# Low part of one weight tile in four made by ScalarE's negated high part and an accumulating DMA, not by VectorE

## The chip, the cores and the metric

The kernel runs on one core of a Trainium2 chip. The core has a matrix engine (TensorE, PE in the profile; its weight loads are PEld), VectorE (DVE), ScalarE (ACT), GpSimd (POOL) and SyncE (SP), which here only issues transfers, and sixteen DMA engines that move data between HBM and SBUF, the on-chip memory. Matrix products land in PSUM. Each engine works through its own queue in order and waits at an instruction until the semaphores named there have come. The metric is the device time of one execution in microseconds (us).

## What is computed

A decoder trunk for 256 tokens of width 2048: one layer of gated linear attention (GLA), one layer of stick-breaking attention, each followed by a SwiGLU block of inner width 5632, and a final norm. Nearly all of the work is in products of the activations with large weight matrices in float32:

```python
a = rmsnorm(h, attn_norm_w[layer])
h = h + gla_mixer(a, gla_w_in, ...)              # layer 0: 2048 x 6160 in, 2048 x 2048 out
# layer 1: a @ sb_w_q, kv @ sb_w_kv, stick-breaking attention, o @ sb_w_out
h = h + swiglu(rmsnorm(h, ffn_norm_w[layer]), ffn_w_gate_up[layer], ffn_w_down[layer])

def swiglu(h, w_gate_up, w_down):
    gate, up = jnp.split(h @ w_gate_up, 2, axis=-1)
    return (jax.nn.silu(gate) * up) @ w_down
```

## The kernel before

The product in float32 is made of three products in the faster format float32r. Each operand is split into a high part, which is the value rounded to 12 bits, and a low part, which is the value minus the high part; hi x hi, hi x lo and lo x hi are summed in PSUM.

All weights come through `load_w` in tiles of 128 x 1024 (512 KB). SP issues the load into a buffer `raw` (line 115), ACT makes `hi` by a rounding copy (line 119), and DVE makes `lo` as raw minus hi (line 120). There are four raw buffers (pool `wraw`) and three each of hi and lo (pool `wsp`). The next load into a raw buffer must wait until it was read for the last time; the next hi and lo must wait until PE has read the old ones. 787 tiles are loaded in all; four of them, in `gemm_tok_in_turn`, have hi and lo in a larger buffer that is handed in as `dst`.

`gemm_tok` uses a tile as the moving operand: two rows of blocks (j), two token tiles (t), three products, so twelve matmuls of 512 columns per tile (line 137). It serves the GLA gate and values, all of the SwiGLU products, the attention values and the output projections. `gemm_col` uses a tile as the stationary operand (lines 169, 170 and 172): sixteen matmuls per tile. It serves q, k and the decay of the GLA layer, and k and q of the attention layer. `inv_rms` makes a small power on POOL (line 211), and `gemm_col` ends with a scaling on POOL (line 176).

The order of the instructions on each engine, and which buffer a tile gets, is laid down by a scheduler when the program is built; it moves matmuls a little against the order of the source.

Of the kernel before, what the change touches and what calls it, by code (L numbers as in the profile page):

```python
# [1 line left out]

# [6 lines left out]
F32 = mybir.dt.float32  # L9
# [4 lines left out]
ALU = mybir.AluOpType  # L14
PSUM = bass.MemoryType.PSUM

P = 128
D = 2048
S = 256
NT = S // P  # L20
# [22 lines left out]
def trunk_kernel(  # L43
# [20 lines left out]
    v, a, pe, g = nc.vector, nc.scalar, nc.tensor, nc.gpsimd  # L64
# [7 lines left out]
    ps_tr = ctx.enter_context(tc.tile_pool(name="ps_tr", bufs=2, space=PSUM))  # L72
    ps_x = ctx.enter_context(tc.tile_pool(name="ps_x", bufs=2, space=PSUM))

    # residual stream, token on the partition
    h = const.tile([P, NT, D], F32, name="h")

    def load_x(nb):
        for t in range(NT):
            nc.sync.dma_start(h[:, t, nb * NB : (nb + 1) * NB], x[t * P : (t + 1) * P, nb * NB : (nb + 1) * NB])  # L80

# [1 line left out]
    ident = const.tile([P, P], F32, name="ident")  # L83
    make_identity(nc, ident)
    ones = const.tile([P, P], F32, name="ones")
# [21 lines left out]
    def gain(key, k):  # L107
        return gains[:, col[key] + k : col[key] + k + 1]

# [1 line left out]
    def load_w(ap, k0, nk, c0, ncol, dst=None):  # L111
        raw = wraw.tile([P, 1024], F32, name="raw")
        hi, lo = dst or (wsp.tile([P, 1024], F32R, name="hi"), wsp.tile([P, 1024], F32R, name="lo"))
        n = nk * ncol
        nc.sync.dma_start(
            raw[:, :n].rearrange("p (k c) -> p k c", k=nk),
            ap[k0 * P : (k0 + nk) * P, c0 : c0 + ncol].rearrange("(k p) c -> p k c", p=P),
        )
        a.copy(hi[:, :n], raw[:, :n])  # L119
        v.tensor_tensor(lo[:, :n], raw[:, :n], hi.bitcast(F32)[:, :n], ALU.subtract)  # L120
        return (hi[:, :n].rearrange("p (k c) -> p k c", k=nk), lo[:, :n].rearrange("p (k c) -> p k c", k=nk))

    def gemm_tok(w_ap, kt, lhs, c0, evac, k_row0=0, before=None):
        """out[token, 512 columns from c0]: activations stationary, weights moving."""
        acc = [ps_acc.tile([P, NB], F32, name="acc") for _ in range(NT)]
        k0 = 0
        while k0 < kt:
            nk = 1 if before is not None and k0 < 2 else 2
            hi, lo = load_w(w_ap, k_row0 + k0, nk, c0, NB)
            if before is not None:  # L130
                before(k0)
            for j in range(nk):
                k = k0 + j
                for t in range(NT):
                    xh, xl = lhs(k, t)
                    for n, (l, r) in enumerate(((xh, hi), (xh, lo), (xl, hi))):
                        pe.matmul(acc[t], l, r[:, j, :], start=(k == 0 and n == 0), stop=(k == kt - 1 and n == 2))  # L137
            k0 += nk
        for t in range(NT):
            evac(t, acc[t])  # L140

    def gemm_tok_in_turn(w_ap, kt, lhs, c0, evac, k_row0):
        """gemm_tok with the block of weights held, so that the first token tile is done before the second."""
        wh, wl = (w.rearrange("p (n a) s c -> p n (a s c)", n=8)[:, i : i + 4] for w in xt_pair()[2:] for i in (0, 4))
        parts = []
        for i, k0 in enumerate(range(0, kt, 2)):
            parts.append(load_w(w_ap, k_row0 + k0, 2, c0, NB, (wh[:, i, :], wl[:, i, :]) if i < 4 else None))
        for t in range(NT):
            acc = ps_acc.tile([P, NB], F32, name="acc")
            for k in range(kt):  # L150
                xh, xl = lhs(k, t)
                hi, lo = (w[:, k % 2, :] for w in parts[k // 2])
                for n, (l, r) in enumerate(((xh, hi), (xh, lo), (xl, hi))):
                    pe.matmul(acc, l, r, start=(k == 0 and n == 0), stop=(k == kt - 1 and n == 2))  # L154
            evac(t, acc)

    def gemm_col(w_ap, c0, nct, xhl, dst, scale):
        """dst[column, 256 tokens] for nct column tiles from c0, times scale: weights stationary, activations moving."""
        nk = 1024 // (nct * P)
        acc = [ps_acc.tile([P, NB], F32, name="acc") for _ in range(nct)]  # L160
        for k0 in range(0, KD, nk):
            hi, lo = load_w(w_ap, k0, nk, c0, nct * P)
            for j in range(nk):
                both = xhl[:, k0 + j].rearrange("p s c -> p (s c)")
                first, last = k0 + j == 0, k0 + j == KD - 1
                for c in range(nct):
                    cs = slice(c * P, (c + 1) * P)
                    if not last:
                        pe.matmul(acc[c], hi[:, j, cs], both, start=first, stop=False)  # L169
                    pe.matmul(acc[c][:, :S], lo[:, j, cs], xhl[:, k0 + j, 0, :], start=False, stop=False)  # L170
                    if last:
                        pe.matmul(acc[c], hi[:, j, cs], both, start=False, stop=True)  # L172
        for c in range(nct):
            a.copy(dst[:, c, :], acc[c][:, S:])
            v.tensor_tensor(dst[:, c, :], acc[c][:, :S], dst[:, c, :], ALU.add)
        g.tensor_tensor(dst, dst, scale.rearrange("p (n c) -> p n c", n=1).broadcast_to([P, nct, S]), ALU.mult)
# [3 lines left out]
        return t[:, :, 0, :], t[:, :, 1, :], t  # L180

    def split_scaled(dst_h, dst_l, src, scale):
        """dst_h + dst_l = src * scale, with scale per partition."""
        a.mul(dst_h, src, scale)  # L184
        v.scalar_tensor_tensor(dst_l, src, scale, dst_h.bitcast(F32), ALU.mult, ALU.subtract)  # L185

    def make_xt(src, nb, dsts):
        """Transposes 512 columns of both token tiles, and splits them times each gain."""
        for j0 in (0, 2):
            tp = ps_tr.tile([P, 512], F32, name="tr")  # L190
            for j in (j0, j0 + 1):
                for t in range(NT):
                    o = (j - j0) * S + t * P
                    pe.transpose(tp[:, o : o + P], src(t)[:, j * P : (j + 1) * P], ident)  # L194
            for j in (j0, j0 + 1):
                k = nb * 4 + j
                for key, kk, xh, xl in dsts:
                    split_scaled(xh[:, k, :], xl[:, k, :], tp[:, (j - j0) * S : (j - j0 + 1) * S], gain(key, kk + (j if key == "gnorm" else k)))
# [3 lines left out]
        a.activation(junk, src, AF.Square, accum_out=ss)  # L202

    def inv_rms(ss, n, name):
        """ss [P, NT, parts] -> (sum / n + eps) ** -0.5, [P, NT]"""
        nt = ss.shape[1]
        s = stat.tile([P, nt], F32, name=f"{name}_s")
        v.tensor_reduce(s, ss, axis=mybir.AxisListType.X, op=ALU.add)
        v.tensor_scalar(s, s, 1.0 / n, EPS, ALU.mult, ALU.add)
        r = stat.tile([P, nt], F32, name=f"{name}_r")  # L210
# [1 line left out]
        return r  # L212

    def along_tokens(r, name):
        """r [token, NT] -> [P, 256], the same row on every partition."""
        dg = stat.tile([P, NT, P], F32, name="diag", bufs=1)
        bp = ps_tr.tile([P, 512], F32, name="tr")
        for t in range(NT):
# [9 lines left out]
        make_xt(lambda t: h[:, t, nb * NB : (nb + 1) * NB], nb, dsts)  # L228

    def residual_gemm(w_ap, kt, lhs, k_row0, after=None, after_tile=None):  # L230
        """h += lhs @ w, 512 columns at a time."""
        for nb in range(NCB):
            def evac(t, acc, nb=nb):
                hs = h[:, t, nb * NB : (nb + 1) * NB]
# [42 lines left out]

                residual_gemm(w_dn, 4 * len(blocks), hid_lhs, blocks[0] * 4, **(after if blocks is PASSES[-1] else {}))

    # ================= layer 0: gated linear attention =================  # L280
    w_in = gla_w_in[0]
    ah, al, ahl = xt_pair()
    a_lhs = lambda k, t: (ah[:, k, t * P : (t + 1) * P], al[:, k, t * P : (t + 1) * P])
# [2 lines left out]
    load_x(0)  # L286

    with tc.tile_pool(name="gla", bufs=1) as gp:
        # output gate input, first block: the input arrives, is summed and transposed alongside
        rg = gp.tile([P, NT, VW], F32, name="rg")  # L290
        ss = stat.tile([P, NT, NCB], F32, name="ss")
        r0 = None
# [24 lines left out]
        rq_bc = stat.tile([P, S], F32, name="rq_bc", bufs=1)  # L317
        v.tensor_scalar(rq_bc, r0_bc, GDK**-0.5, None, ALU.mult)

        # masks within one tile of 128: earlier token by the later halves of a level's blocks, and the diagonal  # L320
        HP = P // 2
        mk = gp.tile([P, len(LEVELS) - 1, HP], U8, name="mk")
        mf = gp.tile([P, HP], F32, name="mf")
# [7 lines left out]
        v.tensor_copy(mk_d, ident)  # L331

        tc.keep_in_program_order(a.preload_act_table_set("natural_log_exp_and_others"))
        # log decay, [key dim, token]
        gl = gp.tile([P, 1, S], F32, name="gl")
        gemm_col(w_in, GIN - P, 1, ahl, gl, r0_bc)
        wgu = gp.tile([P, QKW], F32, name="wgu", tag="vt", bufs=2)
# [17 lines left out]
        for k in range(GKT):  # L355
            v.tensor_tensor_scan(B[:, k, :], B[:, k, :], ab[:, k, :], 0.0, ALU.add, ALU.subtract)  # L356

        # q and k, [key dim, token]
        qt = gp.tile([P, GKT, S], F32, name="qt")
        kt = gp.tile([P, GKT, S], F32, name="kt")  # L360
        for dst, c0, sc in ((qt, 0, rq_bc), (kt, QKW, r0_bc)):
            for pr in range(GKT // 2):
                gemm_col(w_in, c0 + pr * 2 * P, 2, ahl, dst[:, 2 * pr : 2 * pr + 2, :], sc)

        # scores, [earlier token, later token]: pairs split by the smallest aligned block that holds both
        sc_in = gp.tile([P, GH, NT, P], F32, name="sc_in")
        sc_x = gp.tile([P, GH, P], F32, name="sc_x")
        v.memset(sc_in, 0.0)
# [86 lines left out]
    ss = stat.tile([P, NT, NCB], F32, name="ss")  # L455
    ffn(0, fh, fl, r1, after=lambda nb, ss=ss: norm_block(ss, nb, [("kv", 0, kh, kl), ("attn1", 0, qh, ql)]))

    # ================= layer 1: stick-breaking attention =================
    r2 = inv_rms(ss, D, "n")
    r2_bc = along_tokens(r2, "r_bc")  # L460
    rq_bc = stat.tile([P, S], F32, name="rq_bc", bufs=1)
# [3 lines left out]
    with tc.tile_pool(name="sb", bufs=1) as sp_:  # L465
# [5 lines left out]
        v.tensor_copy(tri_r, upto)  # L471
        ones_r = sp_.tile([P, P], F32R, name="ones_r")
        v.tensor_copy(ones_r, ones)
        # two heads side by side: earlier tile 0 with all later tokens, then earlier tile 1 with later tile 1
        ZA, ZW = 2 * S, 3 * S
        pen = sp_.tile([P, ZW], F32, name="pen")
        g.memset(pen, 0.0)
# [12 lines left out]
        def attend(pr, qp):  # L490
# [5 lines left out]
            z = sp_.tile([P, ZW], F32, name="z", bufs=2)  # L496
            v.tensor_tensor(z[:, :ZA], za, pen[:, :ZA], ALU.add)
            v.tensor_tensor(z[:, ZA:], zb[:, :S], pen[:, ZA:], ALU.add)
            # -log_sigmoid(-z) = max(z, 0) + log(1 + exp(-|z|))
            e = sp_.tile([P, ZW], F32, name="e", bufs=2)  # L500
            a.activation(e, z, AF.Abs)
            a.activation(e, e, AF.Exp, scale=-1.0)
# [3 lines left out]
            fl_ = sp_.tile([P, ZW], F32R, name="fl", bufs=2)  # L506
            a.copy(fh_, e)
            v.tensor_tensor(fl_, e, fh_.bitcast(F32), ALU.subtract)
            # sums over the later keys and the key itself
            ca = ps_tr.tile([P, 512], F32, name="tr")  # L510
            cb = ps_tr.tile([P, 512], F32, name="tr")
            pe.matmul(ca, tri_r, fh_[:, :ZA], start=True, stop=False)
# [84 lines left out]
```

## Time and profile before

| | |
|---|---|
| median of 2 runs | 2282.19 us (2281.15 to 2283.24) |
| the profiled execution, first to last instruction | 2279.7 us |
| PE busy | 2263.7 us, 99% |
| PEld busy | 1891.0 us, 83% |
| DVE busy | 1238.5 us, 54% |
| ACT busy | 1046.4 us, 46% |
| POOL busy | 60.4 us, 3% |
| moved by the DMA engines | 419.23 MB, mean 184 GB/s |

The profile is that of one execution. "L120" is line 120 of the kernel. A row of the timeline has its start, its duration, the engine, the line, the operation, what it writes and reads, and in brackets how long the engine was idle before and what ended that. The end of a matmul is modelled: the next one starts before it ends. The granted clock of TensorE stands as a share of full speed.

### The profile page before, as it was taken

To read this page: it belongs to the slowest core of one execution; us is meant where nothing else is said; L and a number is where in the kernel's file an instruction comes from. 1 tells how busy PE (TensorE), PEld (TensorE's weight loads), DVE (VectorE), ACT (ScalarE), POOL (GpSimd) and SP (SyncE) were. 2 spreads that over 40 slices of the span, in tenths; PEclk is the share of its full clock that TensorE was granted. 3 is DMA by queue.
4 is the path that set the end of the run, shared out by engine and by line. 5 is a ranking of instruction groups with operands and counts; after the bars stand their busy time and mean duration, and the time that the engine had idled before them with its cause. 6 is when DMAs were issued, how large, how long until landed. Compare 5 with 4: busy or idle time off the path is not lost.

```text
span 2279.7 us, 27154 instructions
## 1 busy us (share of the span) xinstructions
PE 2263.7 (99%) x10658; PEld 1891.0 (83%) x10658; DVE 1238.5 (54%) x1251; ACT 1046.4 (46%) x1222; POOL 60.4 (3%) x72
## 2 busy tenths in 40 slices
PE   9999999999999999999999999999999999999998
PEld 7888878888888888888888888888888888888887
DVE  6766455545545545544664567655445444554555
ACT  6544444444434443344554446554444344434444
POOL 2100000000000000000000111000000000000000
PEclk9999999999999999999999999999999999999999
DMA  7554555666666666666566654556666666666664
GB/s 224 169 164 143 153 166 181 188 188 190 188 193 193 189 189 193 194 186 193 185 186 194 186 185 141 167 184 191 186 192 190 193 190 192 186 194 193 191 188 157
DMA packets 242712, 419.23 MB, mean 184 GB/s; under 512 B 12972, under 2 KB 64264, under 8 KB 242456
## 3 DMA queue, kind: packets, MB, share of 16 engines
q1 hardware_dynamic: 242408, 416.44, 60.5%
q8 instruction: 83, 1.36, 0.2%
q10 hardware_dynamic: 176, 1.06, 0.1%
q14 instruction: 45, 0.37, 0.0%
HBM read 415.35 MB, written 2.10 MB: 183 GB/s over the span
## 4 chain that ended last, share of the span: by engine, by line
PE 99%; DVE 0%; issue 0%; DMA 0%; ACT 0%; SPq 0%; POOLq 0%; POOL 0%; DVEq 0%; ACTq 0%
PE acc L137 82%; PE acc L169 7%; PE acc L170 4%; PE px L397 1%; PE tr L264 1%; PE tr L194 1%; PE acc L172 0%; PE acc L154 0%; PE px L494 0%; PE tr L525 0%; PE px L439 0%; DMA raw<-in_gla_w_in_dram 0%; DVE B L356 0%; PE px L409 0%; PE tr L526 0%
## 5 line engine op out<-in xcount | busy, mean ns | idle before, releaser
L120 DVE TENSOR_TENSOR lo<-raw,hi 128x1024 fp32r<-128x1024 f32 (+1 forms) x783 | 972.1, 1243 | 938.4 <-ACT hi L119 937.9
L119 ACT CAST hi<-raw 128x1024 fp32r<-128x1024 f32 (+1 forms) x783 | 823.7, 1052 | 1043.1 <-PE acc L137 904.3
L137 PE MATMUL acc<-hi,xhl 128*128 128x512 f32 x4096 | 1274.7, 391 | 0.8 <-ACT xhl L184 0.8
L137 PEld LDWEIGHTS acc<-hi,xhl 128*128 128x128 f32 x4096 | 769.4, 188 | 161.1 <-issue 1.9
L137 PE MATMUL acc<-lo,xhl 128*128 128x512 f32 x2048 | 799.9, 391 | 0.0
L137 PEld LDWEIGHTS acc<-lo,xhl 128*128 128x128 f32 x2048 | 385.1, 188 | 78.7
L137 PE MATMUL acc<-lo,hid_h 128*128 128x512 f32 x680 | 264.9, 390 | 0.0
L137 PE MATMUL acc<-hi,hid_l 128*128 128x512 f32 x680 | 264.6, 389 | 0.0
L169 PE MATMUL acc<-xhl,hi 128*128 128x512 f32 x735 | 256.1, 396 | 0.6 <-ACT hi L119 0.6
L137 PE MATMUL acc<-hi,hid_h 128*128 128x512 f32 x680 | 240.7, 390 | 0.0
L170 PE MATMUL acc<-xhl,lo 128*128 128x256 f32 x784 | 209.6, 281 | 2.1 <-DVE lo L120 2.0
L169 PEld LDWEIGHTS acc<-xhl,hi 128*128 128x128 f32 x735 | 134.8, 188 | 27.7 <-ACT hi L119 1.0
L170 PEld LDWEIGHTS acc<-xhl,lo 128*128 128x128 f32 x784 | 147.7, 189 | 8.8 <-DVE lo L120 3.0
L137 PEld LDWEIGHTS acc<-hi,hid_l 128*128 128x128 f32 x680 | 127.7, 188 | 26.5
L137 PEld LDWEIGHTS acc<-hi,hid_h 128*128 128x128 f32 x680 | 127.6, 188 | 26.3
L137 PEld LDWEIGHTS acc<-lo,hid_h 128*128 128x128 f32 x680 | 127.6, 188 | 26.1
L184 ACT ACTIVATE xhl<-tr,gains 128x256 fp32r<-128x256 f32 x96 | 40.9, 470 | 28.2 <-PE tr L194 20.9
L185 DVE SCALAR_TENSOR_TENSOR xhl<-tr,gains,xhl 128x256 fp32r<-128x256 f32 x96 | 42.4, 478 | 13.0 <-ACT xhl L184 13.0
L235 DVE TENSOR_TENSOR h<-acc,h 128x512 f32<-128x512 f32 x64 | 41.2, 682 | 7.6 <-PE acc L154 5.2
L258 ACT ACTIVATE sg<-acc,n_r 128x512 f32<-128x512 f32 x44 | 30.0, 690 | 20.8 <-PE acc L137 20.8
L267 ACT CAST hid_h<-tr 128x512 fp32r<-128x512 f32 x44 | 23.6, 589 | 31.4 <-PE tr L264 31.4
L268 DVE TENSOR_TENSOR hid_l<-tr,hid_h 128x512 fp32r<-128x512 f32 x44 | 28.3, 686 | 17.3 <-ACT hid_h L267 17.3
(153 smaller groups left out, 709.1 us busy)
## 6 DMA issues: line engine op xcount, KB each, us to landing
raw<-in_ffn_w_gate_up_dram SPq DMA_DIRECT2D x352, 512.0 KB, 3.9
raw<-in_ffn_w_down_dram SPq DMA_DIRECT2D x176, 512.0 KB, 3.7
raw<-in_gla_w_in_dram SPq DMA_DIRECT2D x97, 512.0 KB, 3.9
raw<-in_sb_w_kv_dram SPq DMA_DIRECT2D x64, 512.0 KB, 3.9
raw<-in_gla_w_out_dram SPq DMA_DIRECT2D x32, 512.0 KB, 3.7
raw<-in_sb_w_q_dram SPq DMA_DIRECT2D x32, 512.0 KB, 3.6
raw<-in_sb_w_out_dram SPq DMA_DIRECT2D x32, 512.0 KB, 3.7
h<-in_x_dram SPq DMA_DIRECT2D x8, 256.0 KB, 5.7
```

What stands on the lines that cost most here:

```text
L119: a.copy(hi[:, :n], raw[:, :n])
L120: v.tensor_tensor(lo[:, :n], raw[:, :n], hi.bitcast(F32)[:, :n], ALU.subtract)
L137: pe.matmul(acc[t], l, r[:, j, :], start=(k == 0 and n == 0), stop=(k == kt - 1 and n == 2))
L169: pe.matmul(acc[c], hi[:, j, cs], both, start=first, stop=False)
L170: pe.matmul(acc[c][:, :S], lo[:, j, cs], xhl[:, k0 + j, 0, :], start=False, stop=False)
L184: a.mul(dst_h, src, scale)
L185: v.scalar_tensor_tensor(dst_l, src, scale, dst_h.bitcast(F32), ALU.mult, ALU.subtract)
L194: pe.transpose(tp[:, o : o + P], src(t)[:, j * P : (j + 1) * P], ident)
L235: v.tensor_tensor(hs, acc, hs, ALU.add)
L258: a.activation(sg[t], acc, AF.Silu, scale=r[:, t : t + 1])
L267: a.copy(hh[:, :, ts], tv)
L268: v.tensor_tensor(hl[:, :, ts], tv, hh.bitcast(F32)[:, :, ts], ALU.subtract)
```

## The change

In every fourth tile of those without `dst` (195 of 783), `lo` is no longer made by DVE. ACT writes minus `hi` into `lo`, and POOL then issues a DMA that reads `raw` and adds it to what stands in `lo`. The other tiles are as before. The rest of the diff takes out comments, so that line numbers move by up to seven.

```diff
+from itertools import count
...
+    tiles = count()
+
     def load_w(ap, k0, nk, c0, ncol, dst=None):
         raw = wraw.tile([P, 1024], F32, name="raw")
         hi, lo = dst or (wsp.tile([P, 1024], F32R, name="hi"), wsp.tile([P, 1024], F32R, name="lo"))
...
         a.copy(hi[:, :n], raw[:, :n])
-        v.tensor_tensor(lo[:, :n], raw[:, :n], hi.bitcast(F32)[:, :n], ALU.subtract)
+        if dst is None and next(tiles) % 4 == 3:
+            a.mul(lo[:, :n], hi.bitcast(F32)[:, :n], -1.0)
+            g.dma_start(lo[:, :n], raw[:, :n], accum_op=ALU.add)
+        else:
+            v.tensor_tensor(lo[:, :n], raw[:, :n], hi.bitcast(F32)[:, :n], ALU.subtract)
```

On ACT, at the start of the first product with `ffn_w_down` in layer 0, the casts followed each other before (the numbers tell the tiles apart; hi, lo and raw of one tile have numbers that follow each other):

```order
L119 CAST hi_4685<-raw_4684 128x1024
L119 CAST hi_4703<-raw_4702 128x1024
L119 CAST hi_4721<-raw_4720 128x1024
L119 CAST hi_4739<-raw_4738 128x1024
L119 CAST hi_4761<-raw_4760 128x1024
```

In the changed program the same place on ACT reads:

```order
L122 CAST hi_4734<-raw_4733 128x1024
L124 ACTIVATE lo_4735<-hi_4734 128x1024
L122 CAST hi_4753<-raw_4752 128x1024
L122 CAST hi_4771<-raw_4770 128x1024
L122 CAST hi_4789<-raw_4788 128x1024
L122 CAST hi_4811<-raw_4810 128x1024
L124 ACTIVATE lo_4812<-hi_4811 128x1024
```

Behind every fourth cast now stands the multiplication that writes minus hi into lo, ahead of the next tile's cast.

On PE, the matmuls of that same changed tile (hi_4734, lo_4735) in the changed program, behind the last one of the tile before it (hi_4716):

```order
L144 MATMUL acc_4659<-hi_4716,hid_l_3705 128x512
L144 MATMUL acc_4658<-hi_4734,hid_h_4022 128x512
L144 MATMUL acc_4659<-hi_4734,hid_h_4022 128x512
L144 MATMUL acc_4658<-lo_4735,hid_h_4022 128x512
L144 MATMUL acc_4658<-hi_4734,hid_l_4023 128x512
L144 MATMUL acc_4659<-lo_4735,hid_h_4022 128x512
```

The order is that of the program before at this place (hi, hi, lo, hi, lo); in 166 changed tiles of this form, and in 23 of the form of `gemm_col`, two matmuls with hi stand ahead of the first with lo, in the other six one, and no matmul of a later tile is put between them.

On SP, the loads at the same place before, with the semaphores each waits for (DMAHW is an earlier transfer that SP issued, DVE the last reader of the raw buffer):

```order
L115 DMA raw<-in_ffn_w_down_dram 128x2x512 [waits DMAHW7_49,DVE_49]
L115 DMA raw<-in_ffn_w_down_dram 128x2x512 [waits DMAHW0_49,DVE_49]
L115 DMA raw<-in_ffn_w_down_dram 128x2x512 [waits DMAHW1_49,DVE_49]
L115 DMA raw<-in_ffn_w_down_dram 128x2x512 [waits DMAHW2_49,DVE_49]
L115 DMA raw<-in_ffn_w_down_dram 128x2x512 [waits DMAHW3_49,DVE_49]
```

And now (DMASW is a transfer that POOL issued):

```order
L118 DMA raw<-in_ffn_w_down_dram 128x2x512 [waits DMAHW0_49,DVE_49]
L118 DMA raw<-in_ffn_w_down_dram 128x2x512 [waits DMAHW7_49,DMASW7_49]
L118 DMA raw<-in_ffn_w_down_dram 128x2x512 [waits DMAHW1_49,DVE_49]
L118 DMA raw<-in_ffn_w_down_dram 128x2x512 [waits DMAHW2_49,DVE_49]
L118 DMA raw<-in_ffn_w_down_dram 128x2x512 [waits DMAHW4_49,DVE_49]
L118 DMA raw<-in_ffn_w_down_dram 128x2x512 [waits DMAHW3_49,DMASW0_49]
```

One load in four now waits for an accumulating transfer, and it stands one place later than the buffer's turn would be: the first of these rows is the load of the next changed tile, T+4, into the buffer of T+1, and the second is that of T+5 into the buffer of T.

## Rows read from the trace of the kernel before

**Rows 1.** The page: busy time, share of the span, instructions by engine.

```profile
PE 2263.7 (99%) x10658; PEld 1891.0 (83%) x10658; DVE 1238.5 (54%) x1251; ACT 1046.4 (46%) x1222; POOL 60.4 (3%) x72
```

**Rows 2.** The page: the chain that ended last, by engine.

```profile
PE 99%; DVE 0%; issue 0%; DMA 0%; ACT 0%; SPq 0%; POOLq 0%; POOL 0%; DVEq 0%; ACTq 0%
```

**Rows 3.** Tile lo: who waited for it (us, times).

```profile
who waited for it (us, times):
  PEld acc L170: 3.0, 2
  PE acc L170: 2.0, 1
```

**Rows 4.** Timeline, 600 to 625 us: start, duration, engine, line, operation.

```profile
611.25 0.39 PE L137 MATMUL acc<-hi,hid_l 128*128 128x512 f32 x1
...
611.47 0.39 PE L137 MATMUL acc<-hi,hid_h 128*128 128x512 f32 x1
...
611.67 1.05 ACT L119 CAST hi<-raw 128x1024 fp32r<-128x1024 f32 x1 [1.66 <-PE acc L137]
...
612.76 1.23 DVE L120 TENSOR_TENSOR lo<-raw,hi 128x1024 fp32r<-128x1024 f32 x1 [1.50 <-ACT hi L119]
...
614.19 0.62 PE L137 MATMUL acc<-hi,hid_h 128*128 128x512 f32 x2
...
616.91 0.62 PE L137 MATMUL acc<-hi,hid_h 128*128 128x512 f32 x2
...
617.37 0.39 PE L137 MATMUL acc<-lo,hid_h 128*128 128x512 f32 x1
```

**Rows 5.** Timeline, 1300 to 1312 us, stationary weights.

```profile
1303.70 1.06 ACT L119 CAST hi<-raw 128x1024 fp32r<-128x1024 f32 x1 [1.34 <-PE acc L169]
...
1309.45 0.28 PE L170 MATMUL acc<-xhl,lo 128*128 128x256 f32 x1
```

**Rows 6.** Groups by form: busy us, mean ns of one, idle before.

```profile
L120 DVE TENSOR_TENSOR lo<-raw,hi 128x1024 fp32r<-128x1024 f32 x781 | 970.7, 1244 | 935.7 <-ACT hi L119 935.2
L119 ACT CAST hi<-raw 128x1024 fp32r<-128x1024 f32 x781 | 822.4, 1053 | 1042.5 <-PE acc L137 904.3 <-PE acc L169 98.8 <-ACT xhl L184 17.1
L176 POOL TENSOR_TENSOR kk<-kk,r_bc 128x512 f32<-128x512 f32 x8 | 10.3, 1286 | 166.2 <-DVE kk L175 166.2
L377 ACT ACTIVATE lev<-lev 128x1024 f32<-128x1024 f32 x8 | 8.7, 1085 | 8.3 <-DVE lev L376 8.3
```

**Rows 7.** Tile raw, 600 to 900 us: loads from issue to landing.

```profile
DMA to landing us min/median/max: 3.5/3.8/5.5
```

**Rows 8.** Busy by stretch: PE, PEld, DVE, ACT, POOL, clock, DMA share, GB/s.

```profile
600.00:900.00 300.00, 300.00 (x1346) 248.85 (x1345) 152.14 (x139) 125.30 (x127) 0.00 (x0) 1.00 0.63 190
1700.00:2280.00 580.00, 571.32 (x2554) 473.43 (x2552) 295.03 (x278) 240.23 (x254) 1.10 (x2) 1.00 0.62 188
```

**Rows 9.** DMA issues: number, KB each, median us to landing.

```profile
out_dram<-h SPq DMA_DIRECT2D x8, 256.0 KB, 2.5
fw<-in_final_norm_w_dram ACTq DMA_DIRECT2D x1, 1024.0 KB, 6.0
```

**Rows 10.** Waits of SP's queue: us in total, times, longest.

```profile
SPq L115 <- DVE lo L120: 1785.9, 740, 9.3
```

**Rows 11.** Timeline, 310 to 318 us: the power of the output norm.

```profile
314.70 0.69 POOL L211 TENSOR_TENSOR o_r<-o_s,neg_half 128x2 f32<-128x2 f32 x1 [24.64 <-DVE o_s L209]
315.42 1.41 DVE L444 SCALAR_TENSOR_TENSOR og<-px,o_r,rg 128x512 f32<-128x512 f32 x2 [0.87 <-POOL o_r L211]
```

## The prediction

> **What bounds the kernel now.** I read the engines' busy time first. TensorE (PE) is busy 99% of the span, VectorE (DVE) 54%, ScalarE (ACT) 46%, GpSimd (POOL) 3% [rows 1]; the chain of work that ended last is 99% PE [rows 2]. So time that is taken off DVE shortens nothing by itself: PE sits idle for only 2279.7 - 2263.7 = 16 us in all, and what waited for a low part is 3.0 + 2.0 us [rows 3]. The question is whether the changed tiles come late for PE.
>
> The timeline of a steady stretch shows how early a tile is ready now [rows 4]. A tile's twelve matmuls take 2.72 us (first ones at 611.47, 614.19, 616.91). There are three hi and three lo buffers, so ACT's cast for tile T starts at 611.67, when PE has done the last matmul of tile T-3, begun at 611.25. DVE's subtraction for T follows 0.04 us behind the cast's end and ends at 612.76 + 1.23 = 613.99. PE goes through T-2 and T-1, begins T at 616.91, and takes its first lo at 617.37. From the start of the cast to the first use of lo there are 617.37 - 611.67 = 5.70 us, of which cast and subtraction use 2.32. In the matrices that run with stationary weights the same distance is 1309.45 - 1303.70 = 5.75 us [rows 5]. The cover is therefore some 3.4 us per tile, the same nearly everywhere.
>
> **The change, part by part.** Of 787 weight tiles 195 change. For these, 195 subtractions on DVE go (1.24 us each [rows 6], 242 us in all). This is worth nothing: DVE is idle before them waiting for ACT, and PE does not wait for DVE.
>
> ACT gets 195 multiplications of 128x1024. No row has that form; the cast of the same size takes 1.053 us and an exponential of that size 1.085 [rows 6]. I take 1.06, 207 us in all. It stands right behind the cast of its tile and ahead of the cast of T+1, which may start only 2.72 us after T's; 1.05 + 0.04 + 1.06 = 2.15 fits in, so the other casts are not late. ACT rises to some 1250 us of work, far from a bound.
>
> POOL gets 195 transfers, and lo is now ready when cast, multiplication and transfer have followed each other. The transfer can be issued 1.05 + 0.04 + 1.06 + 0.04 = 2.19 us after the cast's start, so it must land within 5.70 - 2.19 = **3.51 us** of its issue. In 166 of the 195 tiles PE's order has two hi matmuls ahead of the first lo, as at 616.91, and in 23 more of the column form also two; PE's order puts nothing of a later tile in between. What it takes beyond 3.51 us PE stands still for, once per changed tile: PE's queue is in order, and everything behind that lo matmul waits with it. The next changed tile starts from PE's own end of a tile again, so these stops are neither shared nor caught up.
>
> No row shows an accumulating transfer, nor one from SBUF to SBUF, nor one issued by POOL. The nearest are the loads of 512 KB: they land 3.8 us after issue (3.5 to 5.5 in the steady stretch [rows 7]). Their part in the engines: one load per 2.72 us makes a DMA share of 0.63 [rows 8], so a load holds all sixteen engines for 0.63 x 2.72 = 1.71 us, and 3.8 - 1.71 = 2.1 us are issue and completion. An accumulating transfer has raw and -hi to read, 1 MB, so I count its data twice: 2.1 + 2 x 1.71 = 5.5. It shares the engines with the loads, which go on; between nothing and a whole load (1.71) comes on top, half of it is 0.85, together 6.4. The one transfer in the profile that fills 1 MB of SBUF took 6.0 us amid the loads, a 256 KB store 2.5 [rows 9]. I take 6.2, since 1 MB read is what this transfer is nearest to. The lower bound is a plain load, 3.5; the upper one is the longest landing with the data once more and one 128x512 operation of POOL (1.29 us [rows 6]) for making the transfer ready: 5.5 + 1.71 + 1.29 = 8.5.
>
> The Trainium skill (DMA: Bandwidth & Descriptors, Anatomy of one DMA, SWDGE path) gives a DMA of GpSimd some 2.0 us plus its bytes over 436 GB/s. For 512 KB that is an estimate of 3.2 us, by which nothing would be late and the sum would stay at 2282; no run here shows it yet. The skill (Collectives: The Full Stack, The bandwidth ceiling) also says that an adding transfer emits two reads for each write on one ring, which speaks against the change and for counting the data twice; no trace here shows it either.
>
> The loads get a new wait. SP's queue now has the load that reuses a changed tile's raw buffer wait for the transfer, not for DVE, and the buffers change places: load T+4 takes the buffer of T+1, load T+5 that of T. Before, SP waited for DVE's lo in nearly every load (740 times [rows 10]). Counted from T's cast: lo of T+1 is done at 2.72 + 2.32 = 5.04, load T+4 lands at 8.8 (10.5 at the longest), its cast starts at 10.88. The transfer ends at 2.19 + 6.2 = 8.4, load T+5 lands at 12.2 and is wanted at 13.6 plus the stop. The load of T+6 stands behind it on SP for 0.6 us and has more room. So the refill stays hidden; without that cover a late load would cost its whole delay once per four tiles.
>
> POOL runs the small steps of the norms and the scalings of q and k, now with a transfer waiting for ACT in front of them in its queue. Now o_r takes 0.69 us, and DVE waits for it 0.87 us [rows 11]. There are ten such steps; each could be late by a few us, some 40 us at worst. I take nothing; it is inside the range.
>
> **Sum**, against the profiled execution of 2279.7 us: 195 x (6.2 - 3.5) = 195 x 2.7 = 527 us give 2806; the median of the runs lies 2.5 us above the profiled span, which gives **2809 us**.
>
> **Rivals.** *It stays hidden.* If the transfer lands within 3.5 us, as the quickest loads do, PE never waits and the time is 2282; within 2% it stays up to 3.5 + 45.6 / 195 = 3.73 us. For it: the loads' median of 3.8 is only just over the point that decides, and SBUF is at both ends. Against it: twice the data, on engines that are 0.63 busy. The skill's figure above would make it so. Chance 0.09.
>
> *The transfer is far slower than its bytes say,* because the engines add slowly, or because making it ready on POOL takes long. If it were two loads in series at the longest landing, 11.0 us, the stops would be 7.5 us and the time 2282 + 1462 = 3744. Against it: two loads' worth of data per transfer brings the engines only to 6/4 x 0.63 = 0.95 of an undelayed period. A fall of the granted clock during the stops belongs here: all steady rows read 1.00, the level of 2.4 GHz [rows 8]; at 1.2 GHz a tile would take 5.44 us, in the extreme 195 x 10.88 = 2122 us more. Together 0.10.
>
> *DVE's relief pays.* At most the 16 us in which PE is idle can go, 2266 us, which is under 2%; over 2% faster gets 0.01.
>
> **How the numbers follow.** Stops between 0.23 and 5.0 us per changed tile, that is 2282 + 195 x 5.0 = 3257 at the top, hold 0.80 and give the range of 2328 to 3260 us; 0.10 lies above, 0.10 below. Faster by over 2%: 0.01. Within 2%, about what a measurement of this kernel can tell from no change: 0.09. Slower: 0.90.
>
> **What would show it.** In the profile of the changed kernel the chain should hold DMA of lo, and PE should have idle time in front of the lo matmuls of L144 and L177 put down to the transfers, 195 times some 2.7 us, with PE near 81% busy. The list of DMA issues should show lo<-raw on POOL landing after about 6.2 us: near 3.5 the first rival is right, over 8.5 the second. ACT should show L124 195 times near 1.06 us, DVE 592 subtractions. The casts should still wait for PE, not for raw; if they wait for loads, the step on the refill is wrong. The clock should still read 1.00. The prediction is wrong in its main term if PE waits for lo by another amount than the landing time less 3.5 us.

## The result and the profile after

The changed kernel takes **2620.91 us** (median of 2 runs, 2617.75 to 2624.07) against 2282.19 before: a ratio of 1.149, interval 1.145 to 1.152. The profiled execution spans 2622.4 us, 342.7 us more than the 2279.7 of before. The forecast was 2809 us with a range of 2328 to 3260.

The page of the changed kernel: busy time by engine, then the chain that ended last, by engine and by line.

```profile
PE 2338.5 (89%) x10658; PEld 1894.1 (72%) x10658; DVE 1002.5 (38%) x1056; ACT 1247.2 (48%) x1417; POOL 226.3 (9%) x267
...
PE 62%; DMA 33%; ACT 3%; issue 2%; DVE 0%; POOL 0%; SPq 0%; POOLq 0%; DVEq 0%; ACTq 0%
PE acc L144 51%; DMA lo<-raw 32%; PE acc L176 4%; PE acc L177 2%; ACT hi L122 1%; ACT lo L124 1%; PE px L404 1%; PE tr L271 1%; PE acc L161 0%; ACT xhl L191 0%; PE tr L201 0%; PE px L501 0%; PE px L446 0%; ACT junk L209 0%; PE tr L532 0%
```

PE falls from 99% to 89% [rows 1], and the chain, all PE before [rows 2], is now a third transfers of lo. Split by PE's own rows, the 342.7 us are 2622.4 - 2338.5 = 283.9 us idle, 267.9 more than before, and 2338.5 - 2263.7 = 74.8 us of longer busy time (the same matmuls, the first ones behind a stop and those at a lower clock lasting longer).

The waits of the changed kernel (waiting instruction, what ended the wait: us in total, times, longest). PEld is the weight load that stands in front of each matmul:

```profile
PEld acc L144 <- DMA lo<-raw: 310.7, 162, 5.7
PEld acc L177 <- DMA lo<-raw: 33.5, 17, 4.3
...
PE acc L144 <- DMA lo<-raw: 243.5, 157, 5.5
PE acc L177 <- DMA lo<-raw: 26.1, 17, 3.9
```

Before, waits for lo came to 5 us [rows 3]. Now 162 + 17 = 179 of the 195 changed tiles stop PE, and PE's own waits for them, 243.5 + 26.1 = 269.6 us, account for all of its new idle time.

The steady stretch around one changed tile, from the timeline of the changed kernel:

```profile
709.17 1.05 ACT L122 CAST hi<-raw 128x1024 fp32r<-128x1024 f32 x1 [1.62 <-PE acc L144]
...
710.25 1.06 ACT L124 ACTIVATE lo<-hi 128x1024 fp32r<-128x1024 f32 x1
...
711.61 0.87 POOL L125 DMA_DIRECT2D lo<-raw  x1 [11.73 <-ACT lo L124]
711.69 0.62 PE L144 MATMUL acc<-hi,hid_h 128*128 128x512 f32 x2
...
714.41 0.61 PE L144 MATMUL acc<-hi,hid_h 128*128 128x512 f32 x2
...
716.42 0.19 PEld L144 LDWEIGHTS acc<-lo,hid_h 128*128 128x128 f32 x1 [1.82 <-DMA lo<-raw]
716.43 0.50 PE L144 MATMUL acc<-lo,hid_h 128*128 128x512 f32 x1 [1.40 <-DMA lo<-raw]
...
721.77 1.05 ACT L122 CAST hi<-raw 128x1024 fp32r<-128x1024 f32 x1 [1.62 <-PE acc L144]
```

The changed tile T is cast at 709.17, multiplied at 710.25 to 711.31, and its transfer is issued at 711.61. PE reaches T at 714.41 and would want lo 0.46 us later, as in [rows 4], at 714.87. It gets it at 716.43, 4.82 us after the issue: a stop of 1.56 us. The next changed tile's cast starts at 721.77, so four tiles take 12.60 us; four undisturbed ones take 4 x 2.72 = 10.88. The full price of one changed tile here is 1.72 us, and 179 times that is 308 of the 343; a few stops are longer, up to 5.7 us at the weight load.

The groups and the DMA issues of the changed kernel (busy us, mean ns | idle before; then number, KB each, median us to landing), and for tile lo the landing of its transfers:

```profile
L127 DVE TENSOR_TENSOR lo<-raw,hi 128x1024 fp32r<-128x1024 f32 (+1 forms) x588 | 733.7, 1248 | 1494.2 <-ACT hi L122 1494.0
...
L125 POOL DMA_DIRECT2D lo<-raw x195 | 169.5, 869 | 2196.1 <-ACT lo L124 2095.5
...
L124 ACT ACTIVATE lo<-hi 128x1024 fp32r<-128x1024 f32 x195 | 206.6, 1059 | 6.6 <-PE acc L177 1.1
...
raw<-in_ffn_w_gate_up_dram SPq DMA_DIRECT2D x352, 512.0 KB, 4.1
lo<-raw POOLq DMA_DIRECT2D x195, 512.0 KB, 4.8
raw<-in_ffn_w_down_dram SPq DMA_DIRECT2D x176, 512.0 KB, 4.7
...
DMA to landing us min/median/max: 4.5/4.8/7.7
```

The queues of the changed kernel (packets, MB, time as a share of sixteen engines' span). q0 holds the transfers that POOL issues, q1 the loads:

```profile
q1 hardware_dynamic: 242408, 416.44, 49.6%
q0 software_dynamic: 28080, 102.25, 22.1%
```

One transfer occupies all sixteen engines for 0.221 x 2622.4 / 195 = 2.97 us, one load for 0.496 x 2622.4 / 787 = 1.65: the accumulation costs 1.8 loads. Of the 4.82 us to landing, 2.97 are this and 1.85 the rest.

### The profile page after: what moved, and what is told of

It reads as the page before. It is cut to its first block, busy times and chain, and to the rows that moved or that the text cites. A ratio compares the mean times of both kernels' runs of the same rounds, so it can differ in the third digit from the quotient of the medians.

```text
span 2622.4 us, 27734 instructions
## 1 busy us (share of the span) xinstructions
PE 2338.5 (89%) x10658; PEld 1894.1 (72%) x10658; DVE 1002.5 (38%) x1056; ACT 1247.2 (48%) x1417; POOL 226.3 (9%) x267
## 3 DMA queue, kind: packets, MB, share of 16 engines
q0 software_dynamic: 28080, 102.25, 22.1%
q8 instruction: 83, 1.36, 0.2%
q10 hardware_dynamic: 176, 1.06, 0.1%
## 4 chain that ended last, share of the span: by engine, by line
PE 62%; DMA 33%; ACT 3%; issue 2%; DVE 0%; POOL 0%; SPq 0%; POOLq 0%; DVEq 0%; ACTq 0%
PE acc L144 51%; DMA lo<-raw 32%; PE acc L176 4%; PE acc L177 2%; ACT hi L122 1%; ACT lo L124 1%; PE px L404 1%; PE tr L271 1%; PE acc L161 0%; ACT xhl L191 0%; PE tr L201 0%; PE px L501 0%; PE px L446 0%; ACT junk L209 0%; PE tr L532 0%
## 5 line engine op out<-in xcount | busy, mean ns | idle before, releaser
L127 DVE TENSOR_TENSOR lo<-raw,hi 128x1024 fp32r<-128x1024 f32 (+1 forms) x588 | 733.7, 1248 | 1494.2 <-ACT hi L122 1494.0
L144 PE MATMUL acc<-lo,xhl 128*128 128x512 f32 x2048 | 816.6, 399 | 177.0 <-DMA lo<-raw 177.0
L125 POOL DMA_DIRECT2D lo<-raw x195 | 169.5, 869 | 2196.1 <-ACT lo L124 2095.5
L144 PE MATMUL acc<-lo,hid_h 128*128 128x512 f32 x680 | 273.3, 402 | 66.6 <-DMA lo<-raw 66.6
L144 PE MATMUL acc<-hi,hid_h 128*128 128x512 f32 x680 | 249.4, 394 | 0.0
L177 PE MATMUL acc<-xhl,lo 128*128 128x256 f32 x784 | 213.2, 287 | 26.1 <-DMA lo<-raw 26.1
L124 ACT ACTIVATE lo<-hi 128x1024 fp32r<-128x1024 f32 x195 | 206.6, 1059 | 6.6 <-PE acc L177 1.1
```

Source lines behind the costliest of these rows:

```text
L124: a.mul(lo[:, :n], hi.bitcast(F32)[:, :n], -1.0)
L125: g.dma_start(lo[:, :n], raw[:, :n], accum_op=ALU.add)
```

## The experiments

All were timed beside the kernel before on the same chip (2281.6 us; 2281.4 for the last). The theory: every changed tile costs PE what the transfer's landing exceeds the cover, and only that. The cover is the time from the transfer's issue to the matmul that wants lo, here 714.87 - 711.61 = 3.26 us. Its rivals were that something else in the change costs (ACT's extra work, SP's queue, POOL), and that the price comes from contention of the DMA engines.

**The change without its transfer.** ACT negates hi, and DVE adds raw to it:

```diff
-            g.dma_start(lo[:, :n], raw[:, :n], accum_op=ALU.add)
+            v.tensor_tensor(lo[:, :n], raw[:, :n], lo.bitcast(F32)[:, :n], ALU.add)
```

> In every changed tile ACT still writes minus hi into lo, and DVE instead of the accumulating DMA adds raw to it, so only the transfer is undone. Theory (the transfer's landing is the whole cost): cast 1.05, multiplication 1.06 and addition 1.23 us with three hand-overs of 0.04 end 3.4 us after the cast starts, inside the 5.7 us of cover, so PE never waits and the time is that of before, 2282 us within 0.5%. Rival (ACT's 195 multiplications of 1.06 us delay the casts): the time stays above 2282 by a good part of 195 x 1.06 = 207 us, and PE waits for hi.

Measured: 2286.7 us, a ratio of 1.0024 (1.0014 to 1.0033). Its page:

```profile
PE 2265.2 (99%) x10658; PEld 1891.6 (83%) x10658; DVE 1236.9 (54%) x1251; ACT 1247.2 (55%) x1417; POOL 56.5 (2%) x72
```

The ACT part, with the same 1247 us of work on ACT, costs 5 us; the other 334 hang on the transfer.

**A transfer of the same size that doesn't add.**

```diff
-            g.dma_start(lo[:, :n], raw[:, :n], accum_op=ALU.add)
+            g.dma_start(lo[:, :n], raw[:, :n])
```

> The transfer of the changed tiles is issued the same way by POOL but copies raw into lo without adding, so lo is wrong in those tiles; every order and wait is as in the changed kernel. Theory (data read twice: 2.97 us of the engines against 1.65 us of a load): the landing falls from 4.8 to about 3.5 us, and the stop from 1.74 to about 0.4 us, 2282 + 195 x 0.4 = 2360 us. Rival (the landing is mostly what POOL's issue and the completion take, whatever is moved): the landing stays above 4.4 us and the time above 2540 us.

Measured: 2322.7 us, 1.0179 (1.0163 to 1.0194). Landing of its transfers, their queue, and what was left of the waits:

```profile
DMA to landing us min/median/max: 2.8/2.9/6.3
...
q0 software_dynamic: 28080, 102.25, 12.0%
...
PEld acc L144 <- DMA lo<-raw: 25.6, 38, 1.7
PEld acc L177 <- DMA lo<-raw: 13.6, 8, 5.0
```

The same issuer, bytes, place and waits, landing in 2.9 us: under the cover, and 298 of the 339 us are gone. So the price is that of an adding transfer's length, not of having a transfer there. A copy holds the engines for 0.120 x 2316.8 / 195 = 1.43 us, the adding one for 2.97, twice as long. Of the 1.9 us between the two landings 1.54 are this, and the rest agrees with POOL's shorter part, which is busy 0.55 us for each of these issues and 0.87 for an adding one. The landing was expected at 3.5, with a copy priced like a load (1.65) and POOL's part left out. Of the 41 us left, 5 are ACT's part. The weight loads still wait for transfers 46 times, 39 us in all, of which PE itself stands 21; landings went up to 6.3 us, and what made those few long isn't separated.

**Half of the tile through the transfer.**

```diff
-            a.mul(lo[:, :n], hi.bitcast(F32)[:, :n], -1.0)
-            g.dma_start(lo[:, :n], raw[:, :n], accum_op=ALU.add)
+            m = n // 2
+            a.mul(lo[:, :m], hi.bitcast(F32)[:, :m], -1.0)
+            v.tensor_tensor(lo[:, m:n], raw[:, m:n], hi.bitcast(F32)[:, m:n], ALU.subtract)
+            g.dma_start(lo[:, :m], raw[:, :m], accum_op=ALU.add)
```

> In the changed tiles only the first 512 columns go through ACT's negation and the accumulating DMA (256 KB); DVE makes the other 512 by subtraction as before. Theory (landing = 1.85 us of issue and completion + 2.97 us of engine time for a whole tile): 1.85 + 1.49 = 3.3 us, and the multiplication is 0.43 us shorter, so the transfer lands about 0.4 us ahead of the first lo matmul and PE does not wait: 2282 to 2310 us. Rival (fixed cost): landing above 4.4, less 0.43 us, stop about 1 us, some 2480 us.

Measured: 2321.2 us, 1.0174 (1.0157 to 1.0192), 11 us above the upper end expected. Its transfers:

```profile
DMA to landing us min/median/max: 3.2/3.3/6.9
...
q0 software_dynamic: 28080, 51.13, 12.7%
```

Half the bytes hold the engines for 0.127 x 2315.4 / 195 = 1.51 us, half of 2.97, and 1.8 + 1.51 = 3.3 is the landing: the part that doesn't grow with the bytes stays at 1.8. The transfer also goes earlier, since the multiplication and DVE's subtraction each have half the columns and run side by side: 2.01 us behind the cast's start (702.77 to 704.78 in the steady stretch), which makes the cover 5.70 - 2.01 = 3.69. The landing is under it, and the price falls from 1.74 to 0.20 us per tile. The miss is a remainder as large as with the copy, 67 waits of 39 us in all at the weight loads; its cause isn't separated either.

**The lo products last.** In a changed tile all eight matmuls with hi stand ahead of the four with lo, so the cover grows by six matmuls, 6 x 0.227 = 1.36 us, to 4.6. Only `gemm_tok` is changed:

```diff
+            jobs = [(j, t, n) for j in range(nk) for t in range(NT) for n in range(3)]
+            if added[-1]:
+                jobs.sort(key=lambda job: job[2] == 1)
```

> In the changed tiles of the form with moving weights (171 of 195) PE does the eight matmuls with hi first and the four with lo last; the transfer is untouched. Theory (a latency against a fixed cover): the first lo matmul comes 1.81 instead of 0.45 us into its tile, so the cover grows by 1.36 us, the stop falls from 1.74 to about 0.2 to 0.4 us there, and the time to 2621 - 171 x 1.4 = 2380 us; the landing stays at 4.8 us. Rival (the transfers take the DMA engines from the loads, so that PE is fed too slowly whatever the order): the time stays near 2621 us and the wait moves to hi or raw.

Measured: 2388.5 us, 1.0469 (1.0453 to 1.0484). Waits for its transfers, and their landing:

```profile
PEld acc L148 <- DMA lo<-raw: 90.3, 151, 4.1
PEld acc L181 <- DMA lo<-raw: 32.1, 17, 4.4
...
DMA to landing us min/median/max: 4.5/4.8/7.5
```

The transfer is as long as ever; only PE comes to it later, and 232 us go. The wait per stop falls from 310.7 / 162 = 1.92 to 90.3 / 151 = 0.60 us, by 1.32 for 1.36 of added cover. In the column form (L181), left as it was, the wait stays at 32 us. This is the cover theory shown by its other side.

**Four buffers of hi and lo** instead of three, where the storage allows it: the SwiGLU of layer 0, 66 of the 195 changed tiles. ACT may then cast one tile earlier, 2.72 us more of cover. `load_w` takes hi and lo from the pool that stands last in the list `rings`.

```diff
+        with tc.tile_pool(name=f"ffn{layer}", bufs=2) as fp, tc.tile_pool(name=f"ring{layer}", bufs=4 - 3 * layer) as four:
+            if layer == 0:
+                rings.append(four)
```

> In the SwiGLU block of layer 0 (264 of 787 tiles, 66 of them changed) hi and lo have four buffers instead of three; the rest is as in the changed kernel. Theory (latency against cover): there the cast of a tile starts one tile earlier, 2.72 us, more than the stop of 1.74, so PE does not wait in that stretch and the time falls by 66 x 1.74 = 115 us to about 2506 us. Rival (DMA engines bind, or loads come late): the stretch stays as long as in the changed kernel, 2621 us.

Measured: 2492.7 us, 1.0923 (1.0907 to 1.094), 128 us less than the changed kernel, 13 more than expected. From 700 to 1000 us (busy by engine with counts, clock, DMA share, GB/s), first before, then the changed kernel, then with four buffers:

```profile
700.00:1000.00 300.00, 300.00 (x1342) 248.75 (x1341) 150.03 (x136) 125.58 (x127) 0.00 (x0) 1.00 0.63 191
```

```profile
700.00:1000.00 300.00, 263.13 (x1147) 210.44 (x1145) 101.58 (x95) 131.90 (x133) 20.03 (x23) 1.00 0.74 204
```

```profile
700.00:1000.00 300.00, 300.00 (x1342) 248.84 (x1341) 116.88 (x108) 152.87 (x153) 23.52 (x27) 1.00 0.84 238
```

PE does 1147 matmuls in this stretch in the changed kernel, and 1342 with four buffers, as many as before, with the transfers still in it (landing 4.6 to 5.5). At a DMA share of 0.84 the engines carry loads and transfers without a stop: contention is not what costs here, the missing cover is.

**One tile in eight** (`% 8 == 7` in place of `% 4 == 3`), and **two in four** (`% 2 == 1`).

> Only every eighth tile (97 instead of 195) takes the new way. Theory (each changed tile stops PE once, by itself): 2282 + 97 x 1.74 = 2451 us. Rival (the cost comes from a queue or an engine that is overfull only when many transfers are in flight): less than half of the loss, under 2420 us.

Measured: 2472.1 us, 1.0825 (1.0806 to 1.0843): 190.5 us for 97 tiles, 1.96 each, 21 us more than expected. Half of the tiles keep more than half of the loss, so the rival fell. The mean granted clock was 0.991, which accounts for up to 0.009 x 2470.6 = 22 us, not much less than the 29 us of the changed kernel. The trace shows where: in both runs the clock falls only at stops of 2.2 us and more (see below), and this run has 18 of those where the changed kernel has 24. What makes these stops long is open.

> Every second tile (391) takes the new way, with the buffers as they are. Theory (each changed tile stops PE by itself): 2282 + 391 x 1.74 = 2962 us. Rival (the DMA engines bind): two loads and one transfer take 2 x 1.65 + 2.97 = 6.27 us of the engines against 5.44 us of PE work, which alone would give 2282 + 391 x 0.83 = 2607 us; if both add up, or landings lengthen with the traffic, the time lies above 3000 us.

Measured: 2985.7 us, 1.3083 (1.3043 to 1.3122): 704 us for 391 tiles, 1.80 each. Landing of its transfers, and its stretch from 700 to 1000 us:

```profile
DMA to landing us min/median/max: 4.5/6.4/9.3
...
700.00:1000.00 300.00, 242.21 (x985) 188.17 (x986) 61.91 (x60) 134.18 (x133) 35.28 (x41) 0.96 0.83 212
```

This is 24 us above the theory. Here the transfers land 1.6 us later, about one load's engine time, and loads are issued beside them. The price per tile is not much larger for it. A likely reason, not separated by a run: with every second tile changed, the next changed tile's cast starts before the last stop ends (in one place it starts at 706.04, and the stop ends at 707.50), so a stop is also cover for the next. The mean clock was 0.957, up to 0.043 x 2980.6 = 128 us of the 704.

**Both, two in four and four buffers.**

> Every second tile takes the new way, and in the SwiGLU block of layer 0 (264 tiles) hi and lo have four buffers. Theory: with the latency covered, that stretch shows what the DMA engines can carry: two loads and one transfer take 2 x 1.65 + 2.97 = 6.27 us of the engines against 5.44 us of PE work, so a tile takes 3.1 us instead of 2.72 and the DMA share comes near 1.0. Rival (the engines add without taking room from the loads): 2.72 us per tile in that stretch. The other stretches are as with every second tile and three buffers.

Measured: 2832.4 us, 1.2393 (1.2372 to 1.2414). The same stretch, and three of its waits:

```profile
700.00:1000.00 300.00, 275.39 (x1170) 220.68 (x1169) 73.79 (x71) 157.58 (x159) 40.42 (x47) 0.97 0.94 248
...
ACT hi L124 <- DMA raw<-in_ffn_w_gate_up_dram: 38.2, 16, 5.8
PEld acc L146 <- DMA lo<-raw: 33.4, 21, 3.5
PE acc L146 <- DMA lo<-raw: 24.6, 19, 3.1
```

1342 matmuls have become 1170, so a tile takes 2.72 x 1342 / 1170 = 3.12 us, as expected if the DMA engines bind. Casts now wait for loads, and the engines are at a share of 0.94. But that the engines bind isn't shown: their share stays under the 1.0 expected, the clock is at 0.97, and all of PE's 24.6 us of idle time in the stretch are waits for transfers, which land in 6.3 us (median) here, more than even the longer cover of 3.26 + 2.72 = 5.98. What is shown is that more traffic makes the transfers land later; with one tile in four and four buffers they landed in 4.8.

**Six raw buffers** in the SwiGLU of layer 0, so that loads need not wait for the transfers (the same edit as for hi and lo, with `bufs=6 - 5 * layer` for raw).

> In the SwiGLU block of layer 0 (264 tiles, 66 changed) there are six raw buffers instead of four, so that SP's loads no longer stand behind an accumulating transfer. Theory (the transfer lands in 4.8 us because SP's queue holds the loads back while it runs, and the engines are its own): loads now run beside it, its landing in that stretch goes up by part of a load's 1.65 us, at the most to the 6.4 us of the kernel with every second tile, and the time rises by up to 66 x 1.6 = 106 us, to between 2650 and 2727 us. Rival (the engines have room for both, and the landing is what it is by itself): 4.8 us and 2621 us, or less, since loads come earlier.

Measured: 2623.7 us, 1.1493 (1.1473 to 1.1512), as the changed kernel, with a median landing of 4.8 us in that stretch. SP's waits for transfers from 700 to 1000 us, first in the changed kernel, then here:

```profile
SPq L118 <- DMA lo<-raw: 43.0, 23, 2.9
```

```profile
SPq L119 <- DMA lo<-raw: 43.9, 23, 3.0
```

The edit didn't bring about what it was for: SP waits for as many transfers as before. The time and the landing are those that the rival named, but so they would be if nothing had changed, and the run doesn't tell whether the held-back loads are what keeps the engines free for a transfer. That stays open.

## Why the prediction was right, and where its sizes were off

**The bound and the place** were right. PE was the bound; taking 195 subtractions off DVE gave nothing; PE now stands still in front of the first lo matmul of a changed tile, once per tile, neither shared nor caught up. The copy, the half tile, the later lo products and the fourth buffer each take the cost, or most of it, away by one side of the same inequality, landing against cover. That the time lies in the range says less: the range held every stop from 0.23 to 5.0 us, and the measured price of 1.74 us per tile is about two thirds of the 2.7 forecast.

**The landing was too long.** The forecast was 6.2, the measurement 4.8. Counting the data twice was right: 2.97 us of engine time against 1.43 for a copy. Of the 1.4 us too much, 0.45 is in the engine time (2 x 1.71 = 3.42 against 2.97: the data was priced by a load, and a copy is quicker), 0.25 in issue and completion (2.1 against 1.85), and the largest part, 0.7, is the sharing of the engines with loads, the step from 5.5 to 6.2: nothing of it is left in 1.85 + 2.97 = 4.8. The reason can be seen in the changed kernel's windows (busy by engine, clock, DMA share, GB/s) and in the rows of SP's queue at the tile shown above:

```profile
712.00:713.00 1.00, 1.00 (x6) 0.84 (x5) 0.03 (x1) 0.94 (x1) 0.48 (x1) 1.00 0.05 12
713.00:716.00 3.00, 2.02 (x9) 1.33 (x8) 1.51 (x2) 1.05 (x1) 0.00 (x0) 1.00 1.02 180
```

```profile
708.83 0.37 SPq L118 DMA_DIRECT2D raw<-in_ffn_w_down_dram  x1
...
714.23 0.37 SPq L118 DMA_DIRECT2D raw<-in_ffn_w_down_dram  x1
...
716.40 0.91 SPq L118 DMA_DIRECT2D raw<-in_ffn_w_down_dram  x2
```

The transfer is issued at 711.61, and from 712 to 713 the engines are at a share of 0.05; one load joins it late, at 714.23, and two follow as soon as it has landed. Between 709.20 and 714.23 no raw buffer is free for a load: the changed tile's own buffer is held by the transfer, and that of the next tile until DVE has read it, at 712.97 + 1.23 = 714.20. I had the transfer's hold on its raw buffer only as a threat to the loads. In these rows it also keeps the engines clear for the transfer, so a DMA share averaged over the stretch [rows 8] was the wrong measure of what a transfer meets. This is seen, not shown by an experiment: the run with six raw buffers left SP's wait in place. With loads beside it, as in the two-in-four run, the landing was 6.4 and the sharing term a whole load.

The Trainium skill (DMA: Bandwidth & Descriptors, Anatomy of one DMA, SWDGE path) would have made it an estimate of 3.2 us: the copy measured 2.9, near it, but the adding transfer 4.8, so its figure doesn't hold for that kind. What the Trainium skill says of the add in a ReduceScatter (Collectives: The Full Stack, The bandwidth ceiling), two reads for one write on the same ring, agrees with the engine time in the traces, 2.97 us against 1.43; the reads themselves stand in no view.

**The cover was too large.** I gave ACT's hand-over to POOL the 0.04 us that DVE's start takes behind ACT [rows 4]. It is 0.30 (711.31 to 711.61), which makes 3.51 into 3.26. By the sign that the prediction set for its main term, a stop of the landing less 3.5, PE should have stood 1.3 us; it stood 1.56.

**A stop costs more than its length.** The period grows by 1.72 us for a stop of 1.56; the other 0.16 had no term.

Together: 2.7 - 1.4 + 0.25 + 0.16 = 1.7 us per tile, against 343 / 195 = 1.76 measured. The largest single error is the landing's 1.4 us, 273 of the 527 us in the sum; two small ones of the other sign hid 80 of it, which is luck.

**The clock** I had only in a rival. It falls at some places, all of them at the longer stops. One of them, in a row of PE's weight load and the windows around it:

```profile
426.98 0.19 PEld L144 LDWEIGHTS acc<-lo,xhl 128*128 128x128 f32 x1 [2.47 <-DMA lo<-raw]
```

```profile
425.00:427.00 2.00, 0.02 (x1) 0.02 (x1) 1.23 (x1) 0.56 (x1) 0.00 (x0) 1.00 0.84 169
427.00:429.00 2.00, 2.00 (x6) 1.57 (x6) 0.00 (x0) 0.00 (x0) 0.00 (x0) 0.58 0.75 261
429.00:431.00 2.00, 2.00 (x7) 1.57 (x6) 0.00 (x0) 0.00 (x0) 0.00 (x0) 0.56 0.93 330
431.00:433.00 2.00, 2.00 (x10) 1.65 (x9) 0.71 (x1) 1.05 (x1) 0.00 (x0) 1.00 0.33 127
```

After a stop of 2.47 us the granted clock is 0.58 and 0.56 for four microseconds, near the lower level of 1.2 GHz, and then full again; after the usual stop, as at 716.43, it stays at 1.00. Read in windows of 2 us over the whole trace, up to the last few microseconds, the clock falls at 12 stops, of 2.26 to 5.72 us at the weight load, and at none of the shorter ones. Length alone doesn't decide it: another 12 stops, of 2.44 to 3.00 us, have no fall. Over the whole span the mean is 0.989, against 0.999 before: at most 0.011 x 2622.4 = 29 us of the 343.

**The steps priced at nothing.** ACT's 195 multiplications took 1.059 us each (I said 1.06) and delayed nothing that counts: 5 us by the first experiment. The refill stayed hidden: the loads of `ffn_w_down` land in 4.7 us, which was 3.7 before, but ACT's casts wait for loads only twice, 2.0 us in all. Another 60 casts stood 169 us in front of nothing that the profile names (11.7 us before); what held them isn't known, but PE waited for none of them, since its waits for transfers make up all of its new idle time. POOL's small steps were not late. The longest wait for the output norm's power is 0.9 us, as in [rows 11].

**The rivals.** That it stays hidden fell, since the landing was 4.8 and not under 3.73; and the runs whose landings of 2.9 and 3.3 are under the cover show that even then some 40 us remain, close to the 2% at which I had set the border. Far slower fell too: making the transfer ready takes POOL 0.87 us, and that lies within the 4.8. Of DVE's relief nothing came back.

No version here beats the kernel before; the nearest is the one in which DVE does the adding, at 1.0024.

## What to carry to other kernels

An operation moved off a slack engine is judged by one inequality: its latency from the moment its inputs are ready against the time until the bound engine's in-order queue reaches the result; here 4.8 against 3.3 us, and each late tile cost about the difference. Busy shares say nothing about it, and the remedies are a later use (lo products last, -232 us) or an earlier start (a fourth buffer, no stop left in its stretch), not less work elsewhere. An adding transfer counted here as two copies in the DMA engines' time (2.97 against 1.43 us), and so it is to be counted both in its own length and in the engines' budget, which was nearly used up with every second tile changed (share 0.94).

## What the runs showed of the hardware that I had not expected

- An adding SBUF-to-SBUF transfer of 512 KB took 2.97 us of all sixteen DMA engines and landed in 4.8 us; a copy of the same tile 1.43 and 2.9; an adding one of 256 KB 1.51 and 3.3. Beside loads the first landed in 6.4.
- POOL is busy 0.87 us for each adding issue, at 512 KB and at 256 KB (872 ns), and 0.55 us for a copy: what it does for an issue did not grow with the bytes, with the same number of packets for both sizes (28080 in all). It starts 0.30 us behind ACT's end, where DVE starts after 0.04.
- A stop of PE of 2.47 us was followed by four microseconds at a granted clock of 0.57, the usual stop, 1.82 us in the same kind of row, was not. Of the 24 stops of 2.2 us and more 12 had such a fall, and 12 had none.
